# Strassen blocks of a decoder trunk: two pairs of weight tiles multiplied step by step instead of one after the other, a small transpose emitted later, and side banks in another order

## The chip, the core and the metric

The kernel runs on one core of a Trainium2 chip. A core has a matrix engine (TensorE; PE in the profile, with PEld for its loads of the stationary operand), a vector engine (VectorE, DVE), an engine for pointwise functions (ScalarE, ACT), GpSimd (POOL) and SyncE (SP), which here issues nearly all DMA transfers. Matrix products land in PSUM, which has eight banks, each holding one tile of 128 rows and 512 float32 columns. All else lies in SBUF. The metric is the device time of one execution in microseconds (us); lower is better.

## The reference

Two decoder layers over 256 rows of width 2048, all in float32. A layer normalises the rows, projects them (2048 to 9760 columns), runs two kinds of attention side by side, gates and adds them, projects back and adds the residual. Then comes the channel mixer, where the change lies:

```
a = rms_norm(x, n_ffn_pre)
h = (silu(a @ w_gate) * (a @ w_up)) @ w_down      # 2048 -> 5632 -> 2048
return x + rms_norm(h, n_ffn_post)
```

## The kernel before

**Matrix products.** Every float32 operand is split in two parts, `hi` (written by ACT) and `lo` (the remainder, by DVE, line 167 or 256). One product of 128 rows by 512 columns is then three passes on PE: hi by hi, hi by lo, lo by hi (`part`, lines 366 to 368; `product`, lines 400 to 402). A "pass" below is one such matmul of 512 columns. The 256 rows are two tiles of 128, t = 0 and t = 1.

**Weights.** All weights come in "units" of 128 rows by 1024 values, through one queue in the order of use. `emit_raw` issues a unit's DMA on SP into one of five `raw` buffers; `emit_split` makes the two parts in slots of a pool of 37. `ensure(i)` (line 295) is called from the product loops: it splits all units up to i and otherwise at most one further unit per call, as far as 8 units beyond the last finished one; `finish(i)` marks a unit as used up. Instructions are put on the engines' queues in the order in which the program calls for them, and each queue works in that order.

**Side work.** Small jobs (transposes of finished rows, attention heads) are generators. `pump()` (line 321) advances one of them by one step, up to its next `yield`; the product loops call it after every six passes, and so side work comes between products on PE. Side jobs take their PSUM banks in turn from the list `use["side"]`.

**The channel mixer's up half.** Its 5632 columns are 11 chunks of 512 per layer (`ffn(c)`, line 1169). Chunks 0 and 1 are plain: eight gate units, then eight up units. In chunk 0, `turns2` brings the normalised rows; the factor 1/rms of each row is cut into a power of two `p2` and a rest (`powers`, lines 1124 to 1128, on DVE). `spread()` (line 1130) turns the powers of two of both row tiles by a PE transpose (line 1133) into rows and copies them to `rb` (line 1135). `alike(have, j)` (line 1138), called after unit j of the up half, multiplies quarters of the rows' transposed tiles `aT2` by `rb` (line 1146) as soon as their last plain use is over.

Chunks 2 to 10 are "square" (`square_chunk`, line 404; 9 per layer, 18 in all). Gate and up columns are the two halves of one 2 by 2 block product. Of the eight pairs of row tiles of the weights, the first two (`SEVEN = 2`) are multiplied by a Strassen form: seven products instead of eight. For it `split_sums` (line 247) forms sums of the four weight tiles of a pair and splits them, seven slots per pair; the sums of the rows (`smh`, `sml`) are made once per layer. Each of the seven products has an accumulator in a bank of its own. `between(ps)` (line 1202) then combines accumulators 1, 6, 7 and 5: one copy by ACT (line 157) and four additions by DVE (lines 1205 to 1208), all in order. From the third pair on the four plain products accumulate further into the banks of 2, 4, 3 and into an eighth accumulator. `evac` (lines 1213 to 1217) adds the parts, applies silu and the gate. The finished rows `hb` of a chunk are transposed (`h_gen`, line 1100: four PE transposes in one side bank, line 443, then ACT and DVE) during the next chunk, because `between` hands these jobs on (`hand_on`, line 1113).

Of the kernel before, what the change touches and what calls it, by code (L numbers as in the profile page):

```python
# [41 lines left out]
SEVEN = 2  # L42
# [61 lines left out]
def trunk(ctx: ExitStack, tc: tile.TileContext, I: dict, consts: bass.AP, out: bass.AP):  # L104
# [28 lines left out]
    def staged(shape, dt, name, bufs=2):  # L133
        return stage["pool"].tile(shape, dt, tag=name, name=name, bufs=bufs)

    use = {"main": deque(range(4)), "side": deque(range(4, 8))}

    def bank(i, name):
        return banks[i].tile([128, 512], F32, tag="b", name=name)

    def next_bank(kind, name):
        i = use[kind].popleft()
        use[kind].append(i)
        return bank(i, name)
# [4 lines left out]
    def side_ps(name):  # L149
        return next_bank("side", name)  # L150

    def f32(ap):
        return ap.bitcast(F32)
# [74 lines left out]
    units = []  # L228
# [47 lines left out]
    def emit_split(i):  # L276
        u = units[i]
        while st["raw"] < min(i + RAWS, len(units)):
            emit_raw(st["raw"])
            st["raw"] += 1  # L280
        if "block" in u:
            split_sums(u, units[u["block"]])
            return 2
        hi = slot([128, u["per"], u["n"]], F32R, "wh")
        lo = slot([128, u["per"], u["n"]], F32R, "wl")
        split(hi, lo, u.pop("raw"))
        u["hi"], u["lo"] = hi, lo
        return 1
# [6 lines left out]
    def ensure(i):  # L295

        st["seen"] = max(st["seen"], i + 1)
        until = min(st["seen"] + room["ahead"], st["done"] + room["units"], st["split"] + (2 if st["split"] < 24 else 1))
        st["calls"] += 1
        if room["slow"] and st["calls"] % 2:  # L300
            until = 0
        while st["split"] < min(max(i + 1, until), len(units)):
            st["split"] += emit_split(st["split"])

    def finish(i):
        st["done"] = i + 1
        units[i]["hi"] = units[i]["lo"] = units[i]["right"] = None


    side = deque()  # L310
# [10 lines left out]
    def pump(n=1):  # L321
        for _ in range(n):
            while len(side) < width["n"] and waiting:
                side.append(waiting.popleft())
            if not side:
                return
            g = side.popleft()
            if step(g):
                side.append(g)
# [68 lines left out]
    def product(ps, left, right, first, last):  # L398
        (ah, al), (bh, bl) = left, right
        pe.matmul(ps, ah, bh, start=first, stop=False)  # L400
        pe.matmul(ps, ah, bl, start=False, stop=False)  # L401
        pe.matmul(ps, al, bh, start=False, stop=last)  # L402

    def square_chunk(pairs, lhs, sums, between, evac):

        use["side"] = deque([7])
        ps = {i: bank(b, f"acc{i}") for i, b in ((1, 2), (5, 0), (6, 1), (7, 6), (2, 4), (4, 5), (3, 3))}
        for p, (g, u) in enumerate(pairs[:SEVEN]):  # L410
            k1, k2 = 2 * p, 2 * p + 1
            left = {1: lhs(0, k1), 2: lhs(0, k2), 4: lhs(1, k2)}
            left.update({f: sums(i, p) for i, f in enumerate((5, 6, 7, 3))})
            for n, f in enumerate((5, 6, 7, 2, 4, 3, 1)):
                if n % 2 == 0:
                    ensure(u)
                product(ps[f], left[f], units[g]["right"][f - 1], p == 0, p == SEVEN - 1 and f in (1, 5, 6, 7))
            finish(g)
            finish(u)
        between(ps)  # L420
        use["side"] = deque([7, 0, 1, 6])
        ps[8] = bank(2, "acc8")
        last = len(pairs) - 1
        for p in range(SEVEN, last + 1):
            for i, u in enumerate(pairs[p]):
                for t in range(2):
                    if p < last or units[u].get("hi") is None:
                        ensure(u)
                    f = ((2, 4), (3, 8))[i][t]
                    for jj in range(2):  # L430
                        b = units[u]["hi"][:, jj, :], units[u]["lo"][:, jj, :]
                        product(ps[f], lhs(t, 2 * p + jj), b, f == 8 and p == SEVEN and jj == 0, p == last and jj == 1)
                    if t:
                        finish(u)
                    pump()
                    if p == last:
                        evac(t, i, ps[f])
        use["side"], use["main"] = deque([7, 6, 4, 5]), deque(range(4))
# [445 lines left out]
    def run_layer(l, P, aT, rs, turns, x_src, x_mid, x_next):  # L884
# [235 lines left out]
        sums = {}  # L1120
# [7 lines left out]
            dve.tensor_scalar(rest[t].bitcast(I32), r, 0x007FFFFF, 0x3F800000, op0=OP.bitwise_and, op1=OP.bitwise_or)  # L1128

        def spread():  # L1130
            tp = side_ps("rb")
            for t in range(2):
                pe.transpose(tp[:, t * 128:(t + 1) * 128], p2[t].to_broadcast([128, 128]), ident)
            sums["rb"] = staged([128, 2, 128], F32, "rb", 1)
            dve.tensor_copy(sums["rb"], tp[:, 0:256].rearrange("p (t n) -> p t n", t=2))
            yield "rb"

        def alike(have, j):

            if j == 0 or j % 2:  # L1140
                return
            have.need("rb")
            rb, c = sums["rb"], j // 2 - 1
            for t in range(2):
                a = aT2[t][c].rearrange("p k s n -> p (k s) n")
                dve.tensor_tensor(a, f32(a), rb[:, t:t + 1, :].to_broadcast([128, 8, 128]), op=OP.mult)

# [15 lines left out]
            split(hi, lo, sm)  # L1163
            sums["hi"], sums["lo"] = hi, lo

        def lhs_s(i, p):
            return sums["hi"][:, i, p, :], sums["lo"][:, i, p, :]

        def ffn(c):
            hb = staged([128, 2, 512], F32, "hb")  # L1170
            if c < 2:
                ga, ua = P["ffn"][c]
                scale = rest if c else rs2

                def gate_evac(t, p):
                    if c == 0:
                        turns2[t].need("rs")
                        powers(t)
                    act.activation(hb[:, t], p, AF.Silu, scale=scale[t][:, 0:1])

                def up_evac(t, p):
                    dve.scalar_tensor_tensor(hb[:, t], p, scale[t][:, 0:1], hb[:, t], op0=OP.mult, op1=OP.mult)

                if c:
                    chunk(ga, lhs_a2, gate_evac)
                    left_sums()
                    chunk(ua, lhs_a2, up_evac)
                else:
                    chunk(ga, lhs_a2, gate_evac, before=wait_a2, head=8)
                    drain()  # L1190
                    budget(8, 8)
                    have = Once(spread())
                    waiting.append(have)
                    chunk(ua, lhs_a2, up_evac, after=lambda j: alike(have, j))
                    alike(have, 8)
                made_of(c, hb)
                if c == 0:
                    hand_on()
                return
# [11 lines left out]
            def evac(t, right, p):  # L1211
# [4 lines left out]
                else:  # L1216
                    act.activation(o, o, AF.Silu, scale=rest[t][:, 0:1])

            square_chunk(P["ffn"][c], lhs_a2, lhs_s, between, evac)
            made_of(c, hb)  # L1220

# [80 lines left out]
```

## Time and profile before

| | |
|---|---|
| median of 3 runs | 2858.7 us (2858.47 to 2859.44) |
| the profiled execution's own time | 2856.44 us |
| its span, first to last instruction | 2854.6 us |
| PE busy | 2815.7 us, 99% of the span, 13282 matmuls |
| DVE, ACT busy | 1839.9 us (64%), 1394.5 us (49%) |
| DMA | 547 MB, mean 192 GB/s |

A row of a timeline shows when an instruction began, how long it took, its engine, its line, and the tiles that it writes and reads (`out<-in`); in brackets stands how long its engine was idle just before it and whose end it waited for. The end of a matmul is modelled, and neighbouring matmuls overlap: the distance from one start to the next is the measure of PE's pace. In a view of stretches, "PEclk" is the granted TensorE clock as a share of 2.4 GHz.

### The profile page before, as it was taken

To read this page: it belongs to the slowest core of one execution; us is meant where nothing else is said; L and a number is where in the kernel's file an instruction comes from. 1 tells how busy PE (TensorE), PEld (TensorE's weight loads), DVE (VectorE), ACT (ScalarE), POOL (GpSimd) and SP (SyncE) were. 2 spreads that over 40 slices of the span, in tenths; PEclk is the share of its full clock that TensorE was granted. 3 is DMA by queue.
4 is the path that set the end of the run, shared out by engine and by line. 5 is a ranking of instruction groups with operands and counts; after the bars stand their busy time and mean duration, and the time that the engine had idled before them with its cause. 6 is when DMAs were issued, how large, how long until landed. Compare 5 with 4: busy or idle time off the path is not lost.

```text
span 2854.6 us, 35801 instructions
## 1 busy us (share of the span) xinstructions
PE 2815.7 (99%) x13282; PEld 2358.9 (83%) x13282; DVE 1839.9 (64%) x2359; ACT 1394.5 (49%) x2005; POOL 109.0 (4%) x206
## 2 busy tenths in 40 slices
PE   8999999999999999999999999999999999999998
PEld 8988888888788888888899888888878888888886
DVE  6666655556788547875566566655467775478854
ACT  6555654345455435544455455544464444445532
POOL 0100000001000000000011000000020000000000
PEclk9999999999999999999999999999999999999999
DMA  7673446575555655656566635455665555655563
GB/s 235 205 260 120 130 151 205 192 243 185 191 196 182 210 188 192 199 184 218 187 208 223 217 120 154 150 199 190 231 222 180 195 185 195 196 197 183 196 238 115
DMA packets 291231, 547.05 MB, mean 192 GB/s; under 512 B 17200, under 2 KB 59504, under 8 KB 291056
## 3 DMA queue, kind: packets, MB, share of 16 engines
q1 hardware_dynamic: 289424, 543.82, 58.0%
q8 instruction: 104, 1.70, 0.2%
q10 hardware_dynamic: 1632, 0.95, 0.1%
q14 instruction: 71, 0.58, 0.1%
HBM read 536.31 MB, written 8.39 MB: 191 GB/s over the span
## 4 chain that ended last, share of the span: by engine, by line
PE 95%; DVE 2%; ACT 2%; DMA 1%; issue 0%; POOL 0%; SPq 0%; DVEq 0%; ACTq 0%
PE acc L366 21%; PE acc L368 21%; PE acc L367 21%; PE acc L402 8%; PE acc L400 8%; PE acc L401 8%; PE hT L443 1%; PE ph L732 1%; PE ph L731 1%; ACT aT L157 0%; DMA raw<-in_w_ffn_gate 0%; DVE hu L1205 0%; DVE hu L1208 0%; DVE hb L1206 0%; ACT hb L157 0%
## 5 line engine op out<-in xcount | busy, mean ns | idle before, releaser
L167 DVE TENSOR_TENSOR wl<-raw,wh 128x1024 fp32r<-128x1024 f32 (+1 forms) x936 | 1098.7, 1208 | 396.4 <-ACT wh L157 275.5
L157 ACT ACTIVATE wh<-raw 128x1024 fp32r<-128x1024 f32 (+1 forms) x1044 | 1048.7, 1043 | 504.5 <-PE acc L368 103.5
L366 PE MATMUL acc<-wh,aT 128*128 128x512 f32 (+1 forms) x1536 | 601.5, 392 | 2.5 <-ACT wh L157 1.6
L368 PE MATMUL acc<-wh,aT 128*128 128x512 f32 (+1 forms) x1536 | 588.0, 383 | 1.9 <-DVE aT L484 1.8
L367 PE MATMUL acc<-wl,aT 128*128 128x512 f32 (+1 forms) x1536 | 587.8, 383 | 1.1 <-DVE wl L167 1.1
L400 PE MATMUL acc<-wh,aT 128*128 128x512 f32 x972 | 381.4, 392 | 0.0
L402 PE MATMUL acc<-wh,aT 128*128 128x512 f32 x972 | 379.2, 390 | 0.0
L401 PE MATMUL acc<-wl,aT 128*128 128x512 f32 x972 | 378.6, 389 | 0.0
L368 PEld LDWEIGHTS acc<-wh,aT 128*128 128x128 f32 x1536 | 289.4, 188 | 54.2 <-DVE aT L484 4.1
L366 PEld LDWEIGHTS acc<-wh,aT 128*128 128x128 f32 x1536 | 290.2, 189 | 46.8 <-ACT wh L157 2.0
L367 PEld LDWEIGHTS acc<-wl,aT 128*128 128x128 f32 x1536 | 290.2, 189 | 42.9 <-DVE wl L167 1.9
L366 PE MATMUL acc<-wh,hT 128*128 128x512 f32 x704 | 275.0, 391 | 0.0
L368 PE MATMUL acc<-wh,hT 128*128 128x512 f32 x704 | 274.1, 389 | 0.0
L367 PE MATMUL acc<-wl,hT 128*128 128x512 f32 x704 | 273.9, 389 | 0.0
L402 PEld LDWEIGHTS acc<-wh,aT 128*128 128x128 f32 x972 | 182.4, 188 | 38.7
L401 PEld LDWEIGHTS acc<-wl,aT 128*128 128x128 f32 x972 | 182.6, 188 | 37.7
L400 PEld LDWEIGHTS acc<-wh,aT 128*128 128x128 f32 x972 | 182.7, 188 | 37.6
L368 PEld LDWEIGHTS acc<-wh,hT 128*128 128x128 f32 x704 | 132.2, 188 | 27.7
L367 PEld LDWEIGHTS acc<-wl,hT 128*128 128x128 f32 x704 | 132.2, 188 | 27.0
L366 PEld LDWEIGHTS acc<-wh,hT 128*128 128x128 f32 x704 | 132.2, 188 | 27.0
L256 DVE TENSOR_TENSOR wl<-raw,wh 128x1024 fp32r<-128x1024 f32 x108 | 130.8, 1222 | 22.3 <-ACT wh L157 7.4
L366 PE MATMUL acc<-wh,oT 128*128 128x512 f32 x256 | 102.0, 399 | 0.0
(301 smaller groups left out, 2869.1 us busy)
## 6 DMA issues: line engine op xcount, KB each, us to landing
raw<-in_w_in SPq DMA_DIRECT2D x224, 512.0 KB, 4.6
raw<-in_w_ffn_gate SPq DMA_DIRECT2D x176, 512.0 KB, 4.9
raw<-in_w_ffn_up SPq DMA_DIRECT2D x176, 512.0 KB, 4.7
raw<-in_w_ffn_down SPq DMA_DIRECT2D x176, 512.0 KB, 4.8
raw<-in_w_in SPq DMA_DIRECT2D x96, 432.0 KB, 4.4
raw<-in_w_out SPq DMA_DIRECT2D x64, 512.0 KB, 6.3
raw<-in_w_up_nsa SPq DMA_DIRECT2D x32, 512.0 KB, 4.6
raw<-in_w_up_fox SPq DMA_DIRECT2D x32, 512.0 KB, 5.0
```

What stands on the lines that cost most here:

```text
L157: act.activation(o, i, AF.Copy, scale=1.0 if scale is None else scale)
L167: dve.tensor_tensor(lo, src, f32(hi), op=OP.subtract)
L256: dve.tensor_tensor(lo, src, f32(hi), op=OP.subtract)
L366: pe.matmul(ps[t][:, :n], ah, hi, start=first, stop=False)
L367: pe.matmul(ps[t][:, :n], ah, lo, start=False, stop=False)
L368: pe.matmul(ps[t][:, :n], al, hi, start=False, stop=end)
L400: pe.matmul(ps, ah, bh, start=first, stop=False)
L401: pe.matmul(ps, ah, bl, start=False, stop=False)
L402: pe.matmul(ps, al, bh, start=False, stop=last)
L443: pe.transpose(dst[:, j * 128:(j + 1) * 128], s, ident)
L731: pe.matmul(ph[:120, 0:256], b, units[u]["hi"][:, jj, :], start=p == 0, stop=False)
L732: pe.matmul(ph[:120, 0:256], b, units[u]["lo"][:, jj, :], start=False, stop=p == CL - 1)
```

## The change

In `square_chunk` the loops over the two pairs and over the seven products are exchanged: for each product both pairs are multiplied, six passes into one bank, and the products come in the order 6, 5, 7, 1, 2, 4, 3. Both pairs' units are asked for before each product and after it, and all four are marked as finished only at the end of the seven. After that the side list is 7, 1, 6, 0 instead of 7, 0, 1, 6. `spread()` yields six times before its transposes. `alike` does nothing before j = 4 and then handles quarters 0 and 1 together. `lhs_s` takes the product's number instead of a position.

```diff
@@ square_chunk
-        for p, (g, u) in enumerate(pairs[:SEVEN]):
-            k1, k2 = 2 * p, 2 * p + 1
-            left = {1: lhs(0, k1), 2: lhs(0, k2), 4: lhs(1, k2)}
-            left.update({f: sums(i, p) for i, f in enumerate((5, 6, 7, 3))})
-            for n, f in enumerate((5, 6, 7, 2, 4, 3, 1)):
-                if n % 2 == 0:
-                    ensure(u)
-                product(ps[f], left[f], units[g]["right"][f - 1], p == 0, p == SEVEN - 1 and f in (1, 5, 6, 7))
-            finish(g)
-            finish(u)
+        sevens = pairs[:SEVEN]
+        for f in (6, 5, 7, 1, 2, 4, 3):
+            ensure(sevens[-1][1])
+            for p, (g, _) in enumerate(sevens):
+                k1, k2 = 2 * p, 2 * p + 1
+                left = lhs(0, k1) if f == 1 else lhs(0, k2) if f == 2 else lhs(1, k2) if f == 4 else sums(f, p)
+                product(ps[f], left, units[g]["right"][f - 1], p == 0, p == SEVEN - 1 and f in (1, 5, 6, 7))
+            ensure(sevens[-1][1])
+        for u in sevens:
+            finish(u[0])
+            finish(u[1])
         between(ps)
-        use["side"] = deque([7, 0, 1, 6])
+        use["side"] = deque([7, 1, 6, 0])
@@ ffn, chunk 0
         def spread():
+            for _ in range(6):
+                yield
             tp = side_ps("rb")
@@
-            if j == 0 or j % 2:
+            if j < 4 or j % 2:
                 return
             have.need("rb")
-            rb, c = sums["rb"], j // 2 - 1
-            for t in range(2):
+            rb = sums["rb"]
+            for c, t in [(c, t) for c in range(j // 2 - 1 if j > 4 else 0, j // 2) for t in range(2)]:
                 a = aT2[t][c].rearrange("p k s n -> p (k s) n")
@@
-        def lhs_s(i, p):
+        def lhs_s(f, p):
+            i = (5, 6, 7, 3).index(f)
             return sums["hi"][:, i, p, :], sums["lo"][:, i, p, :]
```

## Rows read from the trace of the kernel before

**Rows 1.** The page: the span, the engines' busy time and share, the granted clock in 40 slices (tenths), and the chain that ended last by engine.

```profile
span 2854.6 us, 35801 instructions
PE 2815.7 (99%) x13282; PEld 2358.9 (83%) x13282; DVE 1839.9 (64%) x2359; ACT 1394.5 (49%) x2005; POOL 109.0 (4%) x206
...
PEclk9999999999999999999999999999999999999999
...
PE 95%; DVE 2%; ACT 2%; DMA 1%; issue 0%; POOL 0%; SPq 0%; DVEq 0%; ACTq 0%
```

**Rows 2.** The waits of PE over the whole span, longest first: who waited for whom, us in total, how many times, the longest in us.

```profile
PE rb L1133 <- DVE rest L1128: 11.4, 2, 5.8
PE hT L443 <- DVE hu L1208: 5.5, 16, 0.4
```

**Rows 3.** The timeline of PE where chunk 0 goes from its gate half to its up half, first in layer 0, then in layer 1: the first pass of the up half, its sixth pass, the second transpose of `spread`, the pass after it, and the tenth pass after it.

```profile
717.33 0.39 PE L366 MATMUL acc<-wh,aT 128*128 128x512 f32 x1
...
718.46 0.39 PE L368 MATMUL acc<-wh,aT 128*128 128x512 f32 x1
...
724.80 0.47 PE L1133 MATMUL rb<-ct,p 128*128 128x128 f32 x1 [5.84 <-DVE rest L1128]
724.93 0.78 PE L366 MATMUL acc<-wh,aT 128*128 128x512 f32 x1
...
728.90 0.40 PE L366 MATMUL acc<-wh,aT 128*128 128x512 f32 x1
...
2134.51 0.39 PE L366 MATMUL acc<-wh,aT 128*128 128x512 f32 x1
...
2135.64 0.39 PE L368 MATMUL acc<-wh,aT 128*128 128x512 f32 x1
...
2141.68 0.47 PE L1133 MATMUL rb<-ct,p 128*128 128x128 f32 x1 [5.55 <-DVE rest L1128]
2141.81 0.78 PE L366 MATMUL acc<-wh,aT 128*128 128x512 f32 x1
...
2145.63 0.40 PE L366 MATMUL acc<-wh,aT 128*128 128x512 f32 x1
```

**Rows 4.** The view of stretches, for the nine passes after that transpose in layer 1 and for the time behind them. Columns: the stretch and its length in us, then busy time (instructions) of PE, PEld, DVE, ACT and POOL, the granted clock, the DMA share, GB/s.

```profile
2141.81:2145.63 3.82, 3.82 (x11) 3.00 (x11) 1.56 (x2) 3.18 (x4) 0.00 (x0) 0.53 0.99 334
2145.63:2157.00 11.37, 11.37 (x52) 9.38 (x50) 9.44 (x8) 3.20 (x4) 0.00 (x0) 1.00 0.43 133
```

**Rows 5.** The timelines of ACT and DVE around the same place: what stands ahead of the power of two and the rest of the second row tile in layer 0, and the same last instruction in layer 1.

```profile
722.36 1.06 ACT L157 ACTIVATE wh<-raw 128x1024 fp32r<-128x1024 f32 x1 [3.94 <-DMA raw<-in_w_ffn_gate]
...
723.45 1.23 DVE L167 TENSOR_TENSOR wl<-raw,wh 128x1024 fp32r<-128x1024 f32 x1 [3.29 <-ACT wh L157]
724.59 0.15 DVE L1127 TENSOR_SCALAR p<-rs 128x1 int32<-128x1 int32 x1
724.66 0.14 DVE L1128 TENSOR_SCALAR rest<-rs 128x1 int32<-128x1 int32 x1
...
2141.54 0.14 DVE L1128 TENSOR_SCALAR rest<-rs 128x1 int32<-128x1 int32 x1
```

**Rows 6.** The costliest groups of instructions: the multiplications of the rows' tiles by `rb`. Columns: count, busy us, mean ns of one, idle time of the engine just before them.

```profile
L1146 DVE TENSOR_TENSOR aT<-aT,rb 128x1024 fp32r<-128x1024 f32 x16 | 19.4, 1223 | 8.9 <-PE acc L368 8.2
```

**Rows 7.** The view of stretches (columns as in rows 4) for a square chunk: its 42 Strassen passes; its other 144 passes with eight transposes of `hT` among them; and the 144 other passes of a chunk (chunk 6 of layer 0) that has no transposes. Each stretch runs from the start of its first pass to the start of the pass after its last; a matmul that reaches into it is counted too.

```profile
835.67:845.43 9.76, 9.76 (x44) 7.91 (x42) 7.41 (x8) 3.67 (x4) 0.00 (x0) 1.00 0.55 183
845.43:879.58 34.15, 33.80 (x154) 27.74 (x153) 28.18 (x33) 18.49 (x22) 0.00 (x0) 1.00 0.59 194
1108.65:1141.30 32.65, 32.65 (x146) 27.04 (x145) 27.01 (x31) 17.32 (x20) 0.00 (x0) 1.00 0.54 177
```

**Rows 8.** The timelines of ACT, DVE and PE in the same chunk: ACT's copy of accumulator 1, the first and the last addition of `between`, the pass ahead of the transposes of row tile 0 and the pass after them, and the same for row tile 1.

```profile
845.63 0.60 ACT L157 ACTIVATE hb<-acc 128x512 f32<-128x512 f32 x1 [6.28 <-PE acc L402]
...
846.26 0.69 DVE L1205 TENSOR_TENSOR hu<-acc,hb 128x512 f32<-128x512 f32 x1 [3.07 <-ACT hb L157]
...
848.38 0.69 DVE L1208 TENSOR_TENSOR hu<-acc,hb 128x512 f32<-128x512 f32 x1
...
846.56 0.39 PE L402 MATMUL acc<-wh,aT 128*128 128x512 f32 x1
...
847.14 0.47 PE L400 MATMUL acc<-wh,aT 128*128 128x512 f32 x1
...
848.38 0.40 PE L402 MATMUL acc<-wh,aT 128*128 128x512 f32 x1
849.12 0.66 PE L443 MATMUL hT<-ct,hb 128*128 128x128 f32 x4 [0.35 <-DVE hu L1208]
849.53 0.47 PE L400 MATMUL acc<-wh,aT 128*128 128x512 f32 x1
```

**Rows 9.** The timeline of PE at the head of the 42 Strassen passes of that chunk (the first two).

```profile
835.67 0.40 PE L400 MATMUL acc<-wh,smh 128*128 128x512 f32 x1
835.91 0.40 PE L401 MATMUL acc<-wl,smh 128*128 128x512 f32 x1
```

**Rows 10.** How early the Strassen weights are ready. DVE's last remainders of the second pair for chunk 2 of layer 0, and the first pass of that chunk on PE; ACT's wait for a slot while it splits the second pair of the chunk behind that of rows 7.

```profile
785.78 2.52 DVE L256 TENSOR_TENSOR wl<-raw,wh 128x1024 fp32r<-128x1024 f32 x2
...
791.76 0.40 PE L400 MATMUL acc<-wh,smh 128*128 128x512 f32 x1
...
868.69 1.06 ACT L157 ACTIVATE wh<-raw 128x1024 fp32r<-128x1024 f32 x1 [3.10 <-PE acc L401]
```

## The prediction

> **What bounds the kernel now.** I read the page first. PE is busy 99% of the span at a granted clock of nine tenths or more in every slice, and 95% of the chain that ended last is PE; DVE and ACT are far from full [rows 1]. So a change pays only by what it takes out of PE's own sequence: a gap, passes run at a lower clock, or a longer step from pass to pass. Next come PE's waits: two groups lead, 11.4 us in two waits ahead of the transposes of `rb` and 5.5 us in 16 waits ahead of transposes of `hT` [rows 2]. Both stand at places that the diff touches. The timelines show what these waits cost in all, and the view of stretches shows the step from pass to pass. With 144 passes and no side work a pass takes 32.65 / 144 = 0.2267 us; the 42 Strassen passes take 9.76 / 42 = 0.2324 us [rows 7].
>
> **Part 1: `spread` six steps later.** `pump` runs after every six passes, so `spread` comes onto PE's queue right behind the first six passes of the up half [rows 3]. Its second transpose needs the power of two of row tile 1. DVE makes that behind the remainder of a unit whose first part ACT can only write when a DMA lands (ACT idle 3.94, DVE idle 3.29), and p2 and rest are done at 724.66 + 0.14 = 724.80 [rows 5]. PE stands until then. From the start of the sixth pass to the start of the pass after the transposes it takes 724.93 - 718.46 = 6.47 us in layer 0 and 2141.81 - 2135.64 = 6.17 in layer 1 [rows 3]. Undisturbed, a pass and four transposes take 847.14 - 846.56 = 0.58 [rows 8], which is 0.35 for four transposes; with two I count 0.40. Lost: 6.07 + 5.77 = 11.84 us. Behind the wait the clock is 0.53, close to the 1.2 GHz level, and back at 2.4 GHz after it [rows 4]: the next nine passes take 728.90 - 724.93 = 3.97 and 2145.63 - 2141.81 = 3.82 us [rows 3], against nine at 0.227 plus about 0.06 of settling, 2.10. Lost: 1.87 + 1.72 = 3.59. Together 15.4 us.
>
> After the change the transposes are emitted at the seventh step of the generator, behind seven times six passes of the up half: 717.33 + 42 x 0.2267 = 726.85 and 2134.51 + 9.52 = 2144.03 [rows 3]. The factors are there at 724.80 and 2141.54 + 0.14 = 2141.68 [rows 5], 2.0 and 2.3 us before. What makes them late is a DMA that PE does not pace, so I leave these times. The step that moves issues two transposes on PE and one copy on DVE, no DMA, nothing on POOL or SP. DVE's copy then waits for PE in DVE's queue, ahead of the next remainders; these belong to chunk 1, which begins some 12 us later (16 x 6 passes after 717.33 is 739.1). The quarters of `aT2`: four multiplications of 1.22 us [rows 6] now stand together behind j = 4. j = 4 ends ten times six passes into the half, 13.6 us, and chunk 1 needs the first of the four 8.2 us later. Even with two remainders of 1.23 us [rows 5] ahead all four take 7.3 us, so I count 0; were the cover gone, PE would wait for about one multiplication, 1.2 us per layer. Bounds of part 1: -16 us (the whole wait and the slow passes) to 0 (the wait goes with the transposes).
>
> **Part 2: the side banks.** The first job after `between` takes bank 7, the second took bank 0, where accumulator 5 lies; its last reader is L1208, the fourth addition of `between`. PE has the second set of transposes ready behind twelve passes and waits 0.35 us for that addition [rows 8]. In all it costs more: 849.53 - 848.38 = 1.15 us from pass to pass against 0.58 for the first set, so 0.57 each, and 16 of them are 9.1 us. The check: a chunk's 144 passes with both sets take 34.15 - 32.65 = 1.50 us more than without [rows 7], of which 0.57 is this wait, 0.70 the eight transposes, and the rest settling.
>
> Now the second job takes bank 1, accumulator 6, which L1205 alone reads: the first of the four additions, over 2.1 us before L1208 [rows 8]. That alone exceeds 0.35. Moreover product 1, for which ACT's copy had waited 6.28 us [rows 8], ends after 24 of the 42 passes instead of 42, 18 x 0.23 = 4.1 us earlier. No wait is left there. Bounds: -9.1 to, if only the idle time itself went, -5.5 [rows 2].
>
> **Part 3: six passes to a bank.** The 42 passes have 9.76 - 9.52 = 0.24 us more than at the undisturbed step, 18 x 0.24 = 4.3 us in all [rows 7]. The plain passes, six to a bank, show no such excess, and there the bank changes too. The trace does not tell whether the three-pass change, the other stationary tiles (`smh`) or something else makes it. Bounds: -4.3 (all goes) to, at the slowest step that I see, 835.91 - 835.67 = 0.24 for all 42 [rows 9], 10.08 - 9.76 = 0.32, +5.8 us. Bank changes are halved, so I take half: -2.1.
>
> The Trainium skill, "TensorE: Matmul & The Clock Gate", section "Back-to-back issue gap", gives a spacing that depends only on the columns: at 512 and full clock 512 / 2.4 + 2.5 = 216 ns, with no term for the bank. The trace disagrees with the figure (227 and 232 ns, rows 7). By that rule the exchanged loops are worth nothing; the sum without part 3 is a rival below.
>
> **Part 4: both pairs asked for at once.** The second pair's weights are now needed from the fourth pass on and no longer from the 22nd, 18 x 0.23 = 4.1 us earlier. For chunk 2 of layer 0 DVE ends their last remainders at 785.78 + 2.52 = 788.30, and the chunk begins at 791.76 [rows 10]: 3.5 us in hand, where there were over 8. Later splits wait behind fewer: the cap "eight units beyond the last finished" stays at the chunk's start until all seven products are through, so two units are split after `between` instead of before it (2.1 us of ACT, 2.4 us of DVE at the durations of rows 5), and SP issues the two transfers behind them later as well. These units are first used at the fifth pair, 48 passes or 10.9 us after the seven, and `between` itself now runs earlier by about 4 us in time that DVE spent idle (3.07, rows 8). Slots: those of the first pair were free after 9 to 21 passes, now after 15 to 39; ACT's queue does wait for slots [rows 10], but in the second half of a chunk. I count 0; between -1 and the rival below.
>
> **The sum.** 15.4 + 9.1 + 2.1 = 26.6 us. Against the profiled execution's own time: 2856.44 (span 2854.6 and 1.8 around it) - 26.6 = 2829.8. The median shown is 2.3 us above that execution, so I forecast 2832 us, with its own range of 2828 to 2836.
>
> **The rivals.**
> - The passes stay as they are, so that part of the change doesn't do what it says: the exchange brings no shorter step. For it: no row ties the excess to the bank. Time: 2858.7 - 24.5 = 2834.2.
> - The passes get the slowest step throughout: 24.5 saved, 5.8 paid, 2840. Against it: the mean of the 42 is 0.232 and that of the plain passes 0.227 [rows 7], and the exchanged order is nearer to the plain one.
> - The wait of `spread` comes along: the margin is only 2.0 us against a wait of 5.8, so a DMA 3 us later than in this trace brings a wait back, and with it perhaps the slow passes. Half of part 1 gone: 2840; all of it: 2847.
> - Slower: the second pair's weights become the wait. Place: the fourth pass of each of the 18 square chunks, ahead of which PE's queue stands. If holding pair 1's slots longer (up to 21 passes, 4.8 us) makes the next chunk's splits later by as much plus one DMA, the 3.5 us in hand are gone. Each us beyond costs 18 us. The gain is used up at 26.6 / 18 = 1.5 us of wait per chunk, a slip of 5.0 us. At a slip of 6 us: 18 x 2.5 = 45 us, 2877. Against it: the next chunk's second pair is split some 20 us after the seven products (868.69 against 845.43, rows 7, 10), when both pairs' slots are free.
>
> **How the numbers follow.** Chances: the forecast 0.52, unchanged passes 0.25, slow passes 0.06, the wait of `spread` back in part or whole 0.11, the weights late 0.06 (two thirds of it beyond the break-even). A difference under 0.2% (5.7 us) can't be told from none. Faster holds all but the last case, 0.94; of that case 0.04 is slower and 0.02 within 0.2%. The range 2827 to 2842 holds the first three cases and half of the fourth.
>
> **What would show it.** Step 1 right: no wait of `rb` on rest among PE's waits, and no stretch at 0.53 behind it. Step 2: no wait of `hT` on L1208; the 144 passes at about 33.6 us. Step 3: the 42 passes under 9.76 us. Step 4 wrong: a wait of an `acc` pass with `smh` on a `wl` of line 256 at the head of a chunk. A time above 2842 would mean that one of the two large waits has a successor.

## The result and the profile after

The changed kernel takes 2831.93 us (median of 4 runs, 2831.42 to 2832.14) against 2858.59 us for the kernel before (2857.0 to 2859.44, 4 runs): a ratio of 0.9907, 95% interval 0.989 to 0.9924. The forecast was 2832, in a range of 2827 to 2842. The difference, 26.7 us, lies far above the 0.2% that can be told from none.

The page of the changed kernel (its profiled execution took 2832.00 us) answers to [rows 1]: span, busy time of the engines, chain.

```profile
span 2830.2 us, 35792 instructions
...
PE 2807.9 (99%) x13282; PEld 2358.5 (83%) x13282; DVE 1842.9 (65%) x2359; ACT 1394.9 (49%) x2005; POOL 109.0 (4%) x206
...
PE 98%; ACT 1%; DVE 0%; POOL 0%; issue 0%; DMA 0%; DVEq 0%; SPq 0%; ACTq 0%
```

PE does the same 13282 matmuls. Its share of the chain rose from 95% to 98%: other engines had stood on the chain where PE waited for them. PE's waits, longest first, answer to [rows 2].

```profile
PE gT L1271 <- DMA gp<-in_norm_ffn_pre: 4.3, 1, 4.3
PE acc L368 <- DVE aT L485: 1.8, 3, 0.8
PE acc L366 <- ACT wh L157: 1.3, 1, 1.3
```

Both groups that led before, `rb` on `rest` and `hT` on `hu`, are gone, and no group has come in their place: these three, now the longest, stood in the kernel before too. PE's timeline around the moved transposes in layer 0 answers to [rows 3], and DVE's, with the last piece of the second row tile's factor, to [rows 5].

```profile
727.88 0.39 PE L368 MATMUL acc<-wh,aT 128*128 128x512 f32 x1
728.11 0.38 PE L1136 MATMUL rb<-ct,p 128*128 128x128 f32 x2
728.24 0.48 PE L366 MATMUL acc<-wh,aT 128*128 128x512 f32 x1
...
730.38 0.39 PE L366 MATMUL acc<-wh,aT 128*128 128x512 f32 x1
```

```profile
725.95 0.14 DVE L1129 TENSOR_SCALAR rest<-rs 128x1 int32<-128x1 int32 x1
...
730.01 3.48 DVE L1149 TENSOR_TENSOR aT<-aT,rb 128x1024 fp32r<-128x1024 f32 x3
```

The factor is ready at 725.95 + 0.14 = 726.09, 2.0 us before the transposes at 728.11. The transposes bring no wait, and nine passes behind them take 730.38 - 728.24 = 2.14 us, where they had taken 3.97. The delayed multiplications of `aT` (three of the four of a group shown) come in one block; nothing waits for them.

The view of stretches answers to [rows 7] and [rows 4]: the 42 Strassen passes and the 144 others of the second square chunk, then the passes right behind the two transposes in each layer.

```profile
828.32:838.00 9.68, 9.68 (x43) 7.90 (x42) 8.30 (x11) 3.32 (x4) 0.00 (x0) 1.00 0.50 173
838.00:871.62 33.62, 33.62 (x154) 27.82 (x152) 27.60 (x31) 18.94 (x22) 0.00 (x0) 1.00 0.63 202
...
728.24:730.35 2.11, 2.11 (x12) 1.78 (x11) 2.11 (x4) 1.62 (x3) 0.00 (x0) 1.00 0.90 269
2132.39:2134.50 2.11, 2.11 (x12) 1.78 (x11) 1.94 (x4) 1.61 (x3) 0.00 (x0) 1.00 0.91 288
```

The 144 passes with transposes fell from 34.15 to 33.62 us, the 42 from 9.76 to 9.68, and the granted clock behind `spread` is 1.00 in both layers.

### The profile page after: what moved, and what is told of

The parts are those of the page before. It is cut to its first block, busy times and chain, and to the rows that moved or that the text cites. A ratio compares the mean times of both kernels' runs of the same rounds, so it can differ in the third digit from the quotient of the medians.

```text
span 2830.2 us, 35792 instructions
## 1 busy us (share of the span) xinstructions
PE 2807.9 (99%) x13282; PEld 2358.5 (83%) x13282; DVE 1842.9 (65%) x2359; ACT 1394.9 (49%) x2005; POOL 109.0 (4%) x206
## 4 chain that ended last, share of the span: by engine, by line
PE 98%; ACT 1%; DVE 0%; POOL 0%; issue 0%; DMA 0%; DVEq 0%; SPq 0%; ACTq 0%
PE acc L366 22%; PE acc L368 21%; PE acc L367 21%; PE acc L400 9%; PE acc L402 9%; PE acc L401 9%; PE hT L444 1%; PE ph L733 1%; PE ph L732 1%; PE tp L444 0%; PE no L570 0%; PE no L569 0%; PE no L571 0%; ACT aT L157 0%; PE ns L577 0%; PE ns L576 0%
## 5 line engine op out<-in xcount | busy, mean ns | idle before, releaser
L366 PEld LDWEIGHTS acc<-wh,hT 128*128 128x128 f32 x704 | 132.2, 188 | 26.7
```

The source lines that it names most:

```text
L366: pe.matmul(ps[t][:, :n], ah, hi, start=first, stop=False)
```

## The experiments

Times are medians; the kernel before was run beside each and had 2857.7 to 2858.65 us.

### One part at a time

**Only `spread` and `alike`** (the kernel before with those two hunks).

```diff
         def spread():
+            for _ in range(6):
+                yield
             tp = side_ps("rb")
...
-            if j == 0 or j % 2:
+            if j < 4 or j % 2:
...
```

> The kernel before with the change to spread and alike alone. My theory: the wait of the rb transposes on DVE's rest (11.4 us) and the slow passes behind it (3.6) go, nothing takes their place: 15.4 us less, about 2843; the 16 waits of hT on L1208 stay. Rival (the wait is only moved: the four multiplications together, or DVE's copy held in the queue, make PE wait in chunk 1): a time above 2848 and a new wait of an acc pass on aT or wl near there.

Measured: 2842.44 us (2842.29 to 2842.89), ratio 0.9944, interval 0.9929 to 0.9958, against 2858.42 in the same session: 16.0 us less. PE's waits on `rest` are gone, those on `hu` are all there:

```profile
PE hT L443 <- DVE hu L1210: 5.6, 16, 0.4
```

**Only the list of side banks.**

```diff
-        use["side"] = deque([7, 0, 1, 6])
+        use["side"] = deque([7, 1, 6, 0])
```

> The kernel before with the side list 7, 1, 6, 0 alone. My theory: the second hT job waits for the first addition (L1205) and no longer the fourth, 2.1 us earlier, more than the 0.35 us of the wait, so all 16 waits go: 9.1 us less, about 2849.5. Rival (what frees the job is the earlier end of product 1, the list alone does nothing): 2858, and the waits stay, on another line.

Measured: 2849.98 us (2848.93 to 2850.54), ratio 0.997, interval 0.9958 to 0.9981: 8.4 us less. The waits on `hu` are gone, the two on `rest` stay, and the 144 passes take 33.61 us:

```profile
PE rb L1133 <- DVE rest L1128: 11.2, 2, 5.8
```

```profile
846.84:880.45 33.61, 33.61 (x153) 27.82 (x152) 28.17 (x33) 18.48 (x22) 0.00 (x0) 1.00 0.61 196
```

**Only the exchanged loops** (the changed kernel with the old list and the old `spread` and `alike`).

```diff
-        use["side"] = deque([7, 1, 6, 0])
+        use["side"] = deque([7, 0, 1, 6])
...
-            for _ in range(6):
-                yield
...
```

> The changed kernel with the old side list and the old spread and alike: only the loops are exchanged. My theory: product 1 ends 18 passes earlier, so the fourth addition also ends before the second hT job comes; its waits go without the new list: 9.1 us less, and 1.4 us for the 42 passes (0.08 us in each of 18 chunks, as in the trace of the changed kernel): about 2848. So the two parts cover the same wait and are not additive. Rival (bank 0 is still freed too late): 2857, with the waits on L1208 kept.

Measured: 2847.94 us (2847.63 to 2848.98), ratio 0.9963, interval 0.995 to 0.9976: 10.5 us less. The stretches of its second square chunk:

```profile
835.87:845.54 9.67, 9.67 (x43) 7.90 (x42) 8.29 (x11) 3.31 (x4) 0.00 (x0) 1.00 0.55 174
845.54:879.16 33.62, 33.62 (x153) 27.82 (x152) 27.60 (x31) 18.95 (x22) 0.00 (x0) 1.00 0.63 204
```

The second stretch is as short as with the new list, although the second job still takes bank 0. So the list and the exchange each remove the same 16 waits, and their savings don't add: 16.0 + 8.4 + 10.5 = 34.9, while the whole change saves 26.7. The last addition of `between` shows why, first in the changed kernel, then in this run:

```profile
836.83 0.69 DVE L1212 TENSOR_TENSOR hu<-acc,hb 128x512 f32<-128x512 f32 x1
```

```profile
844.37 0.69 DVE L1210 TENSOR_TENSOR hu<-acc,hb 128x512 f32<-128x512 f32 x1
```

It ends at 837.52, ahead of the end of the 42 passes at 838.00, and here at 845.06, ahead of 845.54. Product 1 is no longer the last of the seven, so `between` runs beside the products that follow it, and bank 0 is free too before the second job asks.

### Why the Strassen passes are slower than others

**Three passes to a bank, the order of products nearly as changed** (the changed kernel with the pair loop outside again; products in the order 6, 5, 7, 3, 1, 2, 4).

```diff
-        for f in (6, 5, 7, 1, 2, 4, 3):
-            ensure(sevens[-1][1])
-            for p, (g, _) in enumerate(sevens):
+        for p, (g, _) in enumerate(sevens):
+            for f in (6, 5, 7, 3, 1, 2, 4):
+                ensure(sevens[-1][1])
...
-            ensure(sevens[-1][1])
```

> The changed kernel with the loop over pairs outside again, so three passes to a bank, but the products in the order 6, 5, 7, 3, 1, 2, 4 in each pair: those with the sums as stationary tile together, those with aT together. Theory of the bank (six passes to a bank make the step shorter): the 42 passes take 9.76 us again, as before the change. Theory of the stationary tile (passes with smh and sml are slow wherever they go, passes with aT are not): 9.68 us as in the changed kernel, within 0.03. Time in both cases within 3 us of 2832.

Measured: 2832.72 us (2832.43 to 2833.07), ratio 0.9909, interval 0.9892 to 0.9926; the 42 passes take 9.74 us.

```profile
828.59:838.33 9.74, 9.74 (x44) 7.90 (x42) 5.69 (x7) 2.95 (x4) 0.00 (x0) 1.00 0.55 178
```

Neither theory holds as it stood. But the starts of the single passes gave the next idea. In the changed kernel a pass with `smh` or `sml` as its stationary tile takes 232.8 ns to the next start on the mean; the 18 passes with `aT`, which now stand in one run, take 227.2. In this experiment `aT` comes in two runs of nine, and its mean is 230.5: each run begins with uneven steps left by the tiles ahead of it (236, 224, 231, 236, 228, 233, 231 ns, then 226). Three passes to a bank don't make these: behind transposes of `hT` in the changed kernel, plain passes, six to a bank, step by 224, 231, 236, 228, 233, 231 ns after their first, before they settle at 226 and 227. The run of 18 in the changed kernel has only the last of these steps, 231, before it settles. So the excess goes with the stationary tile, and partly with what it leaves behind. The build puts `smh` and `sml` at 480 modulo 512 bytes in SBUF (below: the residue of a tile's start address), but the slots that hold the weights and `aT` at 352. (All slices that the passes read are cut from these tiles at multiples of 512 bytes.)

**The same tiles 128 bytes lower.**

```diff
             hu = staged([128, 2, 512], F32, "hu", 1)
+            staged([128, 32], F32, "pad", 1)
```

> The changed kernel with 128 bytes of nothing put ahead of the sums smh and sml, so that these stationary tiles lie at another address modulo 512 bytes (352 instead of 480, the residue that the tiles of aT have); no instruction differs. Passes with smh, sml or wq lock into steps of about 232 ns, those with aT into 226.67. Alignment theory: the step goes with the address modulo 512; the 42 passes fall from 9.68 to about 9.53 us, 18 x 0.15 = 2.7 us less, 2829.2 us. Theory of region or content: the step goes with where in SBUF the tiles lie or with what they hold or with the order of loads; 9.68 us and 2832 us as before.

Measured: 2828.33 us (2828.3 to 2829.14), ratio 0.9896, interval 0.9881 to 0.9911. The 42 passes take 9.52 us, which is 42 x 0.2267, in all 18 chunks, and every step in them is 226 or 227 ns.

```profile
828.45:837.97 9.52, 9.52 (x43) 7.88 (x42) 8.26 (x11) 3.32 (x4) 0.00 (x0) 1.00 0.53 179
```

By that stretch 18 x 0.16 = 2.9 us were due; the medians, from two chips, differ by 3.6, less than the 5.7 us that two medians can tell from none, so the stretch is the surer reading. In the build the one line moves `hu`, `hb` and `rb` by 128 bytes as well as `smh` and `sml`; the next experiment moves the sums alone.

**The sums in two slots of the weights' pool.**

```diff
-            hi = staged([128, 4, SEVEN, 128], F32R, "smh", 1)
-            lo = staged([128, 4, SEVEN, 128], F32R, "sml", 1)
+            hi = slot([128, 4, SEVEN, 128], F32R, "smh")
+            lo = slot([128, 4, SEVEN, 128], F32R, "sml")
```

> The changed kernel with smh and sml in two slots of the weights' pool instead of tiles of their own behind it; the pool is left with two slots fewer for weights during the mixer. Theory of the place (region or alignment): the 42 passes fall from 9.68 to about 9.53 us, 2829.2 us, if the missing slots cost nothing. Theory of content or of the order of loads (what matters is which tile follows which on PE, not where they lie): 9.68 us and 2832 us. If the two missing slots matter, waits of the passes on wl of line 256 appear at the head of square chunks and the time is above 2832 whatever the 42 passes do.

Measured: 2830.39 us (2830.19 to 2830.45), ratio 0.9902, interval 0.9886 to 0.9919. In the build `smh` and `sml` now lie at 352, `hu`, `hb` and `rb` where they were. The 42 passes take 9.52 us in 16 of the 18 chunks, so it is the place of the sums that counts. In two chunks, one per layer, they take 10.14 and 10.16: the missing slots do cost something, though not where I expected it. DVE stood for a slot, with the additions that free product 1's bank queued behind, and PE waited for that bank; the timelines of DVE and of PE in layer 0:

```profile
1260.66 1.23 DVE L167 TENSOR_TENSOR wl<-raw,wh 128x1024 fp32r<-128x1024 f32 x1 [1.01 <-PE acc L401]
...
1264.46 0.68 DVE L1217 TENSOR_TENSOR hu<-acc,hu 128x512 f32<-128x512 f32 x1
```

```profile
1264.49 0.39 PE L402 MATMUL acc<-wh,sml 128*128 128x512 f32 x1
1265.20 0.50 PE L400 MATMUL acc<-wh,aT 128*128 128x512 f32 x1 [0.32 <-DVE hu L1217]
```

**All slots at the sums' residue, 480**, and **all at 0.**

```diff
     junk = cp.tile([128, 512], BF16, name="junk")
+    cp.tile([128, 32], F32, name="fill")
```

```diff
     junk = cp.tile([128, 512], BF16, name="junk")
+    cp.tile([128, 40], F32, name="fill")
...
             hu = staged([128, 2, 512], F32, "hu", 1)
+            staged([128, 120], F32, "pad", 1)
```

> The changed kernel with 128 bytes of nothing ahead of the weights' pool, so that all its slots (weights, aT, hT) move from 352 to 480 modulo 512 bytes, the residue that smh and sml already have. Theory of the difference: what matters is that the stationary tile and the moving tile have the same residue; then the 42 passes fall to 9.52 us, the others stay at 0.2267, some 2828 us as with the pad ahead of smh. Theory of the absolute place: a stationary tile at 480 is slow wherever the moving tile lies; then nearly all passes of the kernel, not only the Strassen ones, go at about 0.232 us, 12,000 x 0.0057 = 70 us more, some 2900 us.

> The changed kernel with 160 bytes ahead of the weights' pool and 480 bytes ahead of smh, so that the slots and the sums all lie at 0 modulo 512 bytes. Theory of the difference: same residue, so 9.52 us for the 42 passes and 2828 us, no more. Theory of the absolute place: a tile that begins on a 512-byte line may be faster than one that begins at 352; the step of all passes would fall below 226.7 ns, at best to the 213.3 ns that 512 columns take at 2.4 GHz, 12,000 x 0.0133 = 160 us less, 2670 us; a step above 226.7 is as possible.

Measured: 2830.1 us (2828.98 to 2830.46), ratio 0.9902, interval 0.9887 to 0.9916; and 2829.47 us (2829.11 to 2830.28), ratio 0.9901, interval 0.9885 to 0.9918. The 42 passes of each:

```profile
827.64:837.16 9.52, 9.52 (x43) 7.88 (x42) 8.25 (x11) 3.32 (x4) 0.00 (x0) 1.00 0.52 173
```

```profile
827.78:837.30 9.52, 9.52 (x43) 7.88 (x42) 8.25 (x11) 3.32 (x4) 0.00 (x0) 1.00 0.59 189
```

So 480 is not slow as such, nor is 0 faster than 352: what counts is that the stationary and the moving tile have the same residue. The step stays at 226.7 ns in all three. The theory of the absolute place, by which the first of the two would have come near 2900 us, falls. The traced spans of the three runs with one residue (the pad, all at 480, all at 0) are 2827.4, 2827.2 and 2827.3 us against 2830.2 in the changed kernel, 2.8 to 3.0 less, as the stretch has it; their medians scatter more (3.6, 1.8 and 2.5 less).

**The pad alone, in the kernel before.** Three passes to a bank, the old order of products, both large waits. The edit is the one line of the pad above.

> The kernel before with the 128 bytes of nothing ahead of smh and sml and nothing else: three passes to a bank, both large waits kept. Theory of the place (stationary and moving tile at different residues modulo 512 are slow, the bank has no part): the 42 passes fall from 9.76 to 9.52 us although the bank still changes every three passes, 18 x 0.24 = 4.3 us, 2854.4 us. Theory of the bank (my part 3): with three passes to a bank part of the excess stays; if the bank's part is the 0.08 us that the exchange took from each chunk, the 42 passes take 9.60 us and the kernel some 2855.8.

Measured: 2854.16 us (2853.17 to 2855.59), ratio 0.9985, interval 0.9976 to 0.9994; 3.9 us less than the 2858.03 of its session. The 42 passes:

```profile
837.54:847.06 9.52, 9.52 (x43) 7.88 (x42) 7.42 (x8) 3.68 (x4) 0.00 (x0) 1.00 0.55 170
```

The bank changes every three passes here, and no excess is left in any of the 18 chunks: a bank change as such costs nothing.

### The late factor, and the slack of the second pair

**Two steps of delay instead of six.**

```diff
-            for _ in range(6):
+            for _ in range(2):
                 yield
```

> The changed kernel with two yields at the head of spread instead of six: the two transposes come behind 18 passes of the up half instead of 42. 18 passes end 4.08 us after the half's start, the second row's factor is there 7.47 us after it in layer 0 and 7.17 in layer 1, so PE should wait 3.4 and 3.1 us. Theory that a late factor is the whole cause: the wait shrinks to that, one for one, 6.5 us lost. If PE's clock falls behind a wait of 3 us as it does behind one of 5.8: 3.6 us more, 2842 us. If the clock only falls behind the longer wait: 2838.5 us. If the factor moves with the transposes (it is late because of where they stand, not because of the DMA): waits near 5.8 and about 2847 us.

Measured: 2840.28 us (2839.51 to 2841.28), ratio 0.9937, interval 0.9922 to 0.9952; 8.3 us over the changed kernel. The second transpose of layer 0, that of layer 1, and the stretches behind each:

```profile
725.39 0.32 PE L1136 MATMUL rb<-ct,p 128*128 128x128 f32 x1 [2.85 <-DVE rest L1129]
...
2132.80 0.32 PE L1136 MATMUL rb<-ct,p 128*128 128x128 f32 x1 [3.08 <-DVE rest L1129]
```

```profile
725.47:727.40 1.93, 1.93 (x9) 1.59 (x10) 1.65 (x3) 1.56 (x3) 0.00 (x0) 1.00 1.03 380
2132.88:2136.84 3.96, 3.96 (x11) 3.11 (x12) 3.68 (x4) 3.24 (x4) 0.00 (x0) 0.57 0.98 328
```

The waits shrank from 5.84 and 5.55 us with no step of delay to 2.85 and 3.08 with two, and with six there is none, so the factor is late by itself and doesn't move with the transposes. Of the two prices for the clock each layer shows one: behind the 2.85 us the passes run at full clock, behind the 3.08 us at 0.57, and the time lies between 2838.5 and 2842.

**Less room for splits made ahead**, in the changed kernel and in the kernel before.

```diff
-                    budget(8, 8)
+                    budget(6, 8)
```

> The changed kernel with room for six instead of eight units beyond the last finished one from the up half of chunk 0 on. The second pair's units of the next square chunk may then be split only when the last plain pair but one is finished, 24 passes or 5.4 us ahead of the chunk; their split takes about 8.4 us on DVE, so its last part is ready some 3 us behind the chunk's start. With both pairs multiplied together the second pair is needed at the fourth pass, 0.7 us in: a wait of about 2.3 us ahead of passes with smh on wl of line 256 in each of 18 chunks, 41 us, some 2873 us. If the second pair's weights are not what limits: 2832 us.

> The kernel before with the same room of six instead of eight units. There the second pair is needed only at the 22nd pass, 4.9 us in, some 2 us after its split is done: no wait at the head of the chunks, 2858 us (my account of the slack). If the pair's order has no part in it, this kernel loses as much as the changed one does with the same room.

Measured: 2831.78 us (2831.47 to 2832.22; ratio 0.9907, interval 0.9891 to 0.9924) and 2857.56 us (2857.2 to 2858.67; ratio 0.9997, interval 0.9988 to 1.0007). Neither moved, and my 41 us for the first of them were wrong. DVE's last remainders of the second pair and the first Strassen pass of chunk 2, first in the changed kernel, then in this one:

```profile
779.10 2.52 DVE L256 TENSOR_TENSOR wl<-raw,wh 128x1024 fp32r<-128x1024 f32 x2
...
785.07 0.40 PE L400 MATMUL acc<-wh,smh 128*128 128x512 f32 x1
```

```profile
781.28 2.52 DVE L256 TENSOR_TENSOR wl<-raw,wh 128x1024 fp32r<-128x1024 f32 x2
...
784.99 0.40 PE L400 MATMUL acc<-wh,smh 128*128 128x512 f32 x1
```

The lead falls from 785.07 - 781.62 = 3.45 to 784.99 - 783.80 = 1.19 us, but it stays a lead, and in none of the other 17 chunks of this run is it shorter. My expectation took the room for a gate in time: that ACT and DVE may begin a split only when PE has finished a unit. It only fixes the order of instructions on the queues, and both engines run ahead of PE on theirs. What the second pair costs once its lead is gone was therefore not tried.

## Why the prediction came out right

**Part 1, `spread`: 15.4 us predicted, 16.0 measured** in the run with that part alone. Its working held where it can be read: a margin of 2.0 us, no wait, nine passes in 2.14 us against 2.10 counted, nothing waiting for the delayed multiplications. The run with two steps of delay shows the mechanism by dose. The factor's time is set by a DMA (in layer 0 ACT stands 4.05 us for it in the changed kernel, 3.94 before), so the two groups of passes put ahead of the transposes, 2.7 us long, took 3.0 and 2.5 us out of the two waits.

**Part 2, the side banks: 9.1 predicted, 8.4 measured** in the run with the list alone. That the cost was the step of 0.57 us from pass to pass and not the 0.35 us of idle time was the right choice between the two bounds. The prediction gave two reasons, the earlier addition and the earlier product 1. Each suffices alone, and the exchange alone removes the waits too. In a change made of several parts, this saving belongs to whichever part is made first.

**Part 3, six passes to a bank: 2.1 predicted; the reason was wrong.** By the stretches it brought 18 x 0.08 = 1.4 us, by the medians of the single parts 26.7 - 16.0 - 8.4 = 2.3; the stretches are the surer reading. The step of the prediction that failed is "Bank changes are halved, so I take half". The excess of 4.3 us was read correctly as a bound, and the pad in the kernel before recovered 3.9 us of it without touching a bank. What the excess hangs on is the relative place in SBUF of the two tiles of a pass. The exchange saved a part of it by another way than I said: it put the 18 passes with `aT` into one run, where they settle (mean step 230.3 ns before, 227.2 after, worked out from their starts), while those with `smh` and `sml` stayed nearly as slow (233.7 and 232.8). The length of the run is not all of it: two runs of nine had 230.5, because they begin with seven uneven steps and the run of 18 with one; what decides that was not tried. The half that I took was near the measured size by chance. The Strassen passes do not "stay as they are", so that rival falls, though its objection, that no row ties the excess to the bank, was sound.

The rule of the Trainium skill that the prediction weighed there ("TensorE: Matmul & The Clock Gate", "Back-to-back issue gap"; given there for isolated matmuls) has no term for the bank. In that it agrees with the pad in the kernel before: 9.52 us with a bank change every three passes. It has no term for the place of the tiles either, and there the runs disagree with it: 9.68 us against 9.52.

**Part 4, both pairs at once: 0 predicted, 0 found.** PE shows no wait for a `wl` of line 256, and the lead in chunk 2, the shortest of the 18, is 3.45 us where the prediction had 3.5. The slower rival did not come. The run with less room took 2.3 us of that lead and the time did not move, so the 1.19 us still in hand were enough; how steep the loss is beyond that stays open.

**The sum.** 26.6 us predicted, 26.7 measured between the medians. Against the profiled execution of before I had 2829.8 and it became 2832.00; the step up to the median of before, 2.3 us, was needed. That the sum comes within 0.1 us is partly luck: part 1 came out 0.6 us above its forecast and part 2 0.7 below, both about the scatter of the medians.

## What to carry to other kernels

When some passes step more slowly than others at the same clock and shape, with no wait in the trace, sort the steps by the tiles they read and compare the addresses of those tiles: 128 bytes of padding were worth 2.9 and 4.3 us by the stretches here, more than the 1.4 that the rewritten loop order brought at that place. A wait of a few us on PE costs its own length and may cost slow passes behind it, so price both from the distance between starts. Where two edits can free the same bank, try each alone before adding their savings.

## What was not expected of the hardware

With fp32r tiles, 128 rows and 512 columns, a pass steps at 226.7 ns when its stationary and its moving tile begin at the same residue modulo 512 bytes (0, 352 and 480 were tried), and at 232.8 to 233.7 ns on the mean when the residues are 480 and 352. Whether 512 or 256 is the unit can't be told from these runs, and why the place matters stays open; no experiment had another difference than 128 bytes. The slow steps leave a trail: passes with equal residues behind them, or behind transposes, need one to nine steps of 224 to 236 ns to settle, and where there are four or more the last four are nearly the same each time (236, 228, 233, 231).

A wait of 3.08 us left PE at a granted clock of 0.57 for the next passes, and one of 2.85 us in the same execution left it at 1.00.
